# A decoder layer's kernel: first-norm squares on ScalarE, low parts on VectorE, weight sums in a fixed order, two more warming matmuls

## Chip, cores and metric

One core of one Trainium2 chip runs the kernel. The metric is the device time of one execution in microseconds (us), lower is better; each kernel is given by the median of its runs.

## What is computed

One decoder layer serves 528 prompt tokens (512 and 16 learned meta tokens) and 32 sample tokens, 560 columns in all; everything is fp32. Cut to what matters here:

```python
def swiglu(x, w_gate, w_up, w_down):
    return (jax.nn.silu(x @ w_gate) * (x @ w_up)) @ w_down

h = x + 0.5 * swiglu(rmsnorm(x, ffn1_norm), ffn1_w_gate, ffn1_w_up, ffn1_w_down)
n = rmsnorm(h, mix_norm)
# attention over a compressed cache for the one half of the heads, a
# causal convolution for the other, and one output projection
h = h + mix
h = h + 0.5 * swiglu(rmsnorm(h, ffn2_norm), ffn2_w_gate, ffn2_w_up, ffn2_w_down)
y = rmsnorm(h, final_norm)
```

The model width is 1024 and the hidden width of each FFN 2816, that is 22 hidden tiles of 128.

## The kernel before

**Stages.** The first FFN runs from the start to about 420 us, the mixers (projections, attention, convolution, output projection) to about 793 us, the second FFN to about 1180 us. Activations lie transposed, features on partitions and tokens along the row. A tile of 560 tokens (544 in the second FFN) goes to TensorE (PE) in two halves of 280 (272).

**Split products.** An fp32 product is made of three matmuls: the weights are split into a high part `wh`, a copy that ScalarE (ACT) rounds, and a low part `wl`, the weights less `wh`; the tokens likewise (`xs` and `xc`, two parts in one tile). The matmuls are high by high, high by low and low by high. There are three buffers each for `wh` and `wl`. In `w_split` (L272) the copy is L286 and the low part L287, on GpSimd (POOL).

**Plain hidden tiles.** Each FFN takes its hidden tiles in groups of 8, 7 and 7, and behind each group adds the down projection of the group to `h`. The first 5 tiles of the first FFN and the first 4 of the second are plain: gate and up times all 8 token tiles, 96 matmuls a tile; `evict` multiplies by the norm's factor (L184), takes silu (L752) and the product `hv` (L756), and splits it into `hid`: high part on ACT (L757), low part on POOL (L758). During them `Combos` (L594) makes the token combinations that the other tiles need: normed tokens `xn` (L621), sums `xt` (L627), and their splits `xc` (ACT L607, VectorE, DVE, L608).

**Seven-product units.** The other 17 and 18 hidden tiles, 35 units, use a Strassen-like scheme (`seven_unit`, L649): seven products m0 to m6 of 12 matmuls each take the place of eight. Four of the seven weight operands are tiles as loaded or corner differences, three are sums kept in the tile `ws`. `seven(i, m)` (L292) splits the operand of product m (`wh` on ACT L299, `wl` on DVE L300) and then makes the next sum on DVE (L308): sum 0 is `ws = a21 + a22`, sum 1 `ws -= a11`, sum 2 `ws = a12 - ws`, sum 3 `a11 -= a21`. Product 1 uses `ws` after sum 0, product 2 after sum 1, product 3 after sum 2; product 4 uses a11 after sum 3. PSUM results that a later product adds to are copied out first: `snap` (ACT, tile `sn`, L668) after products 0, 1 and 2. At a unit's end stand additions (DVE L672), silu (ACT L691), `hv` (two halves, DVE L696) and the split of `hid` (ACT L698, DVE L699).

**Order of the work.** The program emits its instructions piece by piece and a scheduler sets their order on each engine, by its own estimate of durations; a manual dependency without a semaphore (`add_manual_dep`) only fixes an order. On the chip each engine then works off its own queue in that order. SyncE issues the weight loads.

**First norm.** The start makes the split of the 8 token tiles (`feed`: ACT L542, DVE L543), and the sum of their squares in `Split.square`: squares of even tiles on POOL (L510) and of odd ones on ACT (L512), added on DVE (L521). The matmuls of the first hidden tiles need only the split tokens; from the sum, `rsqrt` (L425, p1 on PE L430, Newton step L462 to L466) and `spread` (L474, p2 on PE L481, copies to `rb` L483 and L485) make the norm's factor, which every eviction of a plain tile and every `xn` waits for. `NORM0` sets after how much of the plan's time PE turns to p1. `warm` (L468) runs matmuls on constants before the first weights are there.

Of the kernel before, what the change touches and what calls it, by code (L numbers as in the profile page):

```python
# [7 lines left out]
F32 = mybir.dt.float32  # L8
# [7 lines left out]
KD = 8  # L16
# [27 lines left out]

NORM0 = 12.5
NORM_LAT = 2.2
# [64 lines left out]
def kernel(  # L111
# [95 lines left out]
    def col(c):  # L207
        return par[:, c:c + 1]


    stream = []

    first_new = set()

    def add_w(ap, n):
        stream.append((ap, n))

    def add_ffn(gu, dn, apart=0, plain=NF):
        f0 = 0
        for nf in GROUPS:  # L220
            for f in range(f0, f0 + nf):
                if f == plain:
                    first_new.add(len(stream))
                add_w(gu[f], 2048 if f < plain else 0)
            for d in range(KD - (apart if f0 + nf == NF else 0)):
                add_w(dn[d, :, 128 * f0:128 * (f0 + nf)], 128 * nf)
            f0 += nf

    add_ffn(f1_gu, f1_d, 0, PLAIN1)
    for c in PLAN:  # L230
# [6 lines left out]
    for d, e in [(d, 1) for d in range(KD)] + [(d, 0) for d in range(KD)]:  # L237
        add_w(w_out_t[d, :, 512 * e:512 * e + 512], 512)
    add_ffn(f2_gu, f2_d, 2, PLAIN)

# [32 lines left out]
    def w_split(upto):  # L273
        while st["split"] < min(upto, len(subs)):
# [11 lines left out]
            nc.scalar.activation(out=hi, in_=raw, func=AF.Copy)  # L286
            nc.gpsimd.tensor_tensor(out=lo, in0=raw, in1=hi.bitcast(F32), op=ALU.subtract)  # L287
            splits[j] = (hi, lo)
# [3 lines left out]
    def seven(i, m):  # L292
# [213 lines left out]

    def square(part, after=None, pool=False):
        sq = Tm([128, part.shape[-1]], "sq")
        if pool:
            ins = nc.gpsimd.tensor_tensor(out=sq, in0=part, in1=part, op=ALU.mult)  # L510
        else:
            ins = nc.scalar.activation(out=sq, in_=part, func=AF.Square)  # L512
        if after is not None:
            tc.add_manual_dep(ins.ins, after.ins.name, mybir.DependencyInfo(
                mybir.DependencyClass.NoSync, mybir.DependencyReason.DATA), reason="the products wait for less")
# [11 lines left out]
    def hk(k):  # L527
        return hs[k // 2][:, k % 2]

    class Split:  # L530
# [9 lines left out]
        def feed(self, k, square=True):  # L540
            xk = U("x", [128, 2, self.n], F32R, "xs")
            fed = nc.scalar.activation(out=xk[:, 0], in_=hk(k), func=AF.Copy, scale=col(self.g + k))  # L542
            nc.vector.scalar_tensor_tensor(  # L543
                out=xk[:, 1], in0=hk(k), scalar=col(self.g + k), in1=xk[:, 0].bitcast(F32), op0=ALU.mult, op1=ALU.subtract
            )
            self.x[k] = xk
            if square:
                self.square(k)
            return fed

        def square(self, k, after=None, pool=False):
            self.ssum = accumulate(self.ssum, hk(k), after, pool)
            if k == KD - 1 and self.g != P_FIN:
# [95 lines left out]
    def seven_unit(w, cb, n, hid):  # L649
# [44 lines left out]
        for a, ps in ((0, b1), (1, b2)):  # L694
# [3 lines left out]
        nc.scalar.activation(out=x[:, 0], in_=hv, func=AF.Copy)  # L698
        lo = nc.vector.tensor_tensor(out=x[:, 1], in0=hv, in1=x[:, 0].bitcast(F32), op=ALU.subtract)  # L699
        tc.add_manual_dep(lo.ins, last_sum[0].ins.name, mybir.DependencyInfo(  # L700
            mybir.DependencyClass.NoSync, mybir.DependencyReason.DATA), reason="the next products wait for the sum")
        hid.append(x)

    def ffn(xs, hook, tail=None, plain=NF):
# [7 lines left out]
        for gi, nf in enumerate(GROUPS):  # L712
            hid = []
            for f in range(nf):
# [9 lines left out]
                for kh in range(2):  # L724
                    for j in range(2):
# [3 lines left out]
                        for k in range(4 * kh, 4 * kh + 4):  # L729
# [4 lines left out]
                            if plain < NF and xs.ev.ready:  # L734
# [580 lines left out]
    def main():  # L1315
# [461 lines left out]
```

## Time and profile before

| | |
|---|---|
| runs | 1204.67, 1199.27, 1201.39 us; median 1201.39 |
| profiled execution | 1197.67 us, its span 1195.9 us |
| mean granted clock of TensorE | 0.976 of full speed |
| busy: PE | 1133.9 us (95%) |
| DVE | 792.3 us (66%) |
| ACT | 535.0 us (45%) |
| POOL | 379.2 us (32%) |
| chain that ended last | PE 80%, DVE 10%, issue 3% |

The span is from the first to the last instruction; the profiled execution's own time is 1.8 us more. Busy is the share of the span in which an engine had an instruction under way. Matmuls overlap, so a busy PE can still be a PE that runs below its best pitch. The chain is followed back from the last instruction, at each step to what released it.

### The profile page before, as it was taken

Reading aid. Unit: us, or ns where it says so; the run is one execution under the profiler, and the core shown is the slowest. Engines: PE = TensorE matmul, PEld = TensorE weight load, DVE = VectorE, ACT = ScalarE, POOL = GpSimd, SP = SyncE. Lnnn points to the kernel's source line nnn. Section 1 sums busy time; section 2 is a strip of 40 time slices with the busy share of each in tenths; the row PEclk is TensorE's granted clock in tenths of the full one; section 3 lists DMA queues with packets and bytes.
Section 4 is the critical chain, followed back from the end, with each engine's and each line's share of the span. In section 5 each row is a group of like instructions: output and inputs, shape, how many; then the busy total and the mean of one; then the engine's idle time right before and its main releaser. Section 6 shows DMA issues by size and latency. Waiting matters only on the chain.

```text
span 1195.9 us, 24540 instructions
## 1 busy us (share of the span) xinstructions
PE 1133.9 (95%) x9314; PEld 1032.3 (86%) x9314; DVE 792.3 (66%) x1537; ACT 535.0 (45%) x1119; POOL 379.2 (32%) x374
## 2 busy tenths in 40 slices
PE   7999999999999999987889999999899999999995
PEld 7989999999999987876545556999899999999994
DVE  6898138834884346999877465659981598168824
ACT  4445226533655414432534555444552355245631
POOL 5440420033004545577434323444214100410141
PEclk8999999999999989998979999999899999999997
DMA  4151322332226656987869884223233233323222
GB/s 159 63 167 61 108 65 84 107 111 78 89 74 211 199 175 196 305 262 232 272 224 315 308 286 158 80 89 98 89 125 90 68 106 102 101 66 104 67 69 75
DMA packets 91062, 168.60 MB, mean 141 GB/s; under 512 B 18976, under 2 KB 25120, under 8 KB 90944
## 3 DMA queue, kind: packets, MB, share of 16 engines
q1 hardware_dynamic: 88352, 162.27, 42.4%
q0 software_dynamic: 2048, 4.20, 1.2%
q8 instruction: 74, 1.21, 0.4%
q10 hardware_dynamic: 544, 0.56, 0.1%
q14 instruction: 44, 0.36, 0.1%
HBM read 161.33 MB, written 5.65 MB: 140 GB/s over the span
## 4 chain that ended last, share of the span: by engine, by line
PE 80%; DVE 10%; issue 3%; ACT 2%; DMA 2%; POOL 2%; SPq 0%; another core or an unknown queue 0%; DVEq 0%; POOLq 0%; ACTq 0%
PE mm L349 36%; PE mm L661 31%; PE sc L1045 3%; PE ob L1067 2%; PE po L1292 2%; PE s L1236 2%; DVE cacc L917 1%; PE pt L1276 1%; DVE xc L608 1%; POOL wl L287 1%; PE mm L1607 1%; DVE wl L300 1%; DMA out<-glu 1%; PE p L481 1%; DVE xt L627 1%
## 5 line engine op out<-in xcount | busy, mean ns | idle before, releaser
L287 POOL TENSOR_TENSOR wl<-wr,wh 128x512 fp32r<-128x512 f32 (+1 forms) x177 | 229.9, 1301 | 541.8 <-ACT wh L286 530.7
L661 PE MATMUL mm<-xc,wh 128*128 128x272 f32 (+1 forms) x1960 | 371.9, 290 | 1.1 <-ACT wh L299 0.9
L661 PEld LDWEIGHTS mm<-xc,wh 128*128 128x128 f32 x1960 | 306.6, 188 | 1.8 <-ACT wh L299 1.3
L661 PE MATMUL mm<-xc,wl 128*128 128x272 f32 (+1 forms) x980 | 281.5, 293 | 3.6 <-DVE wl L300 3.6
L349 PE MATMUL mm<-hid,wh 128*128 128x280 f32 (+1 forms) x1352 | 226.9, 289 | 1.8 <-ACT wh L286 1.8
L286 ACT ACTIVATE wh<-wr 128x512 fp32r<-128x512 f32 (+1 forms) x177 | 107.9, 612 | 251.7 <-PE mm L349 194.9
L349 PEld LDWEIGHTS mm<-hid,wh 128*128 128x128 f32 x1352 | 192.6, 188 | 2.0 <-ACT wh L286 2.0
L661 PEld LDWEIGHTS mm<-xc,wl 128*128 128x128 f32 x980 | 182.2, 188 | 9.8 <-DVE wl L300 9.8
L349 PE MATMUL mm<-xs,wh 128*128 128x280 f32 (+2 forms) x992 | 181.8, 303 | 8.5 <-DVE xs L543 3.5
L349 PEld LDWEIGHTS mm<-xs,wh 128*128 128x128 f32 (+1 forms) x992 | 150.5, 196 | 14.0 <-DVE xs L543 4.2
L782 DVE SCALAR_TENSOR_TENSOR h<-mm,h 128x280 f32<-128x280 f32 (+1 forms) x92 | 36.8, 441 | 165.9 <-PE mm L349 165.9
L349 PE MATMUL mm<-hid,wl 128*128 128x280 f32 (+1 forms) x676 | 140.9, 290 | 0.0
L349 PE MATMUL mm<-xs,wl 128*128 128x280 f32 (+2 forms) x496 | 114.3, 305 | 6.1 <-POOL wl L287 6.0
L299 ACT ACTIVATE wh<-ra 128x512 fp32r<-128x512 f32 x140 | 87.8, 629 | 71.5 <-PE mm L661 62.8
L349 PEld LDWEIGHTS mm<-hid,wl 128*128 128x128 f32 x676 | 106.4, 188 | 0.0
L300 DVE TENSOR_TENSOR wl<-ra,wh 128x512 fp32r<-128x512 f32 x140 | 99.7, 715 | 3.9 <-ACT wh L299 1.1
L299 ACT ACTIVATE wh<-ws 128x512 fp32r<-128x512 f32 x105 | 66.2, 630 | 76.5 <-DVE ws L308 36.3
L349 PEld LDWEIGHTS mm<-xs,wl 128*128 128x128 f32 (+1 forms) x496 | 83.2, 196 | 10.3 <-POOL wl L287 8.7
L300 DVE TENSOR_TENSOR wl<-ws,wh 128x512 fp32r<-128x512 f32 x105 | 73.7, 702 | 26.9 <-ACT wh L299 24.3
L917 DVE SCALAR_TENSOR_TENSOR cacc<-glu,par,cacc 128x512 f32<-128x512 f32 x120 | 89.9, 749 | 1.5
L998 POOL DMA_INDIRECT rope<-in_pool_r,pr_sb x64 | 63.7, 996 | 46.4 <-PE sc L1045 33.5
L668 ACT ACTIVATE sn<-mm 128x272 f32<-128x272 f32 (+1 forms) x105 | 40.9, 390 | 29.2 <-PE mm L661 29.2
(247 smaller groups left out, 1514.4 us busy)
## 6 DMA issues: line engine op xcount, KB each, us to landing
page<-in_pool_c SPq DMA_DIRECT2D x256, 256.0 KB
ra<-in_f_gu SPq DMA_DIRECT2D x70, 512.0 KB
wr<-in_f_d SPq DMA_DIRECT2D x62, 256.0 KB
wr<-in_f_gu SPq DMA_DIRECT2D x36, 256.0 KB
wr<-in_w_in_t SPq DMA_DIRECT2D x24, 256.0 KB
wr<-in_f_d SPq DMA_DIRECT2D x30, 192.0 KB
wr<-in_w_out_t SPq DMA_DIRECT2D x16, 256.0 KB
h<-in_x_t SPq DMA_DIRECT2D x8, 280.0 KB
```

The costliest lines, as they stand in the source:

```text
L286: nc.scalar.activation(out=hi, in_=raw, func=AF.Copy)
L287: nc.gpsimd.tensor_tensor(out=lo, in0=raw, in1=hi.bitcast(F32), op=ALU.subtract)
L299: nc.scalar.activation(out=hi, in_=w, func=AF.Copy)
L300: nc.vector.tensor_tensor(out=lo, in0=w, in1=hi.bitcast(F32), op=ALU.subtract)
L349: nc.tensor.matmul(out=ps[a][:m, 0:n], lhsT=w, rhs=x[:, a * n:(a + 1) * n], start=first and o == 0 and j == 0, stop=last and o == 1,)
L661: nc.tensor.matmul(out=ps, lhsT=w_[:, c], rhs=x, start=first and k == 0 and j == 0, stop=k == 3 and j == 2, skip_group_check=True)
L668: nc.scalar.activation(out=s, in_=src, func=AF.Copy)
L782: last = halves(lambda o, i, x: nc.vector.scalar_tensor_tensor(out=o, in0=i, scalar=0.5, in1=x, op0=ALU.mult, op1=ALU.add), hk(d), ps, hk( ...
L917: last_tap = nc.vector.scalar_tensor_tensor(out=ps, in0=g[:, tp:S0 + tp], scalar=w, in1=ps, op0=ALU.mult, op1=ALU.add)
L998: last = nc.gpsimd.indirect_dma_start(out=rope[:, pg], out_offset=None, in_=pool_r, in_offset=bass.IndirectOffsetOnAxis(ap=pr_sb[:, 32 * g ...
L1045: nc.tensor.matmul(out=ps[32 * b:32 * b + 32], lhsT=w[:, g, 32 * b:32 * b + 32], rhs=x, start=(i_ == 0), stop=(i_ == 2), tile_position=(0, ...
L1067: nc.tensor.matmul(out=ob[32 * b:32 * b + 32, :], lhsT=pts[:, 128 * pg + 32 * b:128 * pg + 32 * b + 32], rhs=tiles[b][:, pg, 0:256], start ...
```

## The change

Five edits. `NORM0` goes from 12.5 to 15.5 and `warm(12)` to `warm(14)`. The squares of the first norm are all made on ACT, behind the split of the last token tile, and their additions on DVE stand behind the last low part of the tokens. Of the plain tiles' weights, those of tiles 2 to 4 of the first FFN and 1 to 3 of the second (`prepared`, 12 low parts in each FFN) get their `wl` on DVE, not on POOL, and so do the low parts of those tiles' `hid` (3 in each). The last three calls of `cb.last` (the last token combinations) come a little earlier. In the seven-product units a new helper, `behind`, fixes one order on DVE: every low part behind the previous sum, and every sum behind the low part emitted before it, so `last_sum` is now a chain through all of them.

```diff
-NORM0 = 12.5
+NORM0 = 15.5
...
+    def behind(ins, *others):
+        for o in others:
+            if o is not None:
+                tc.add_manual_dep(ins.ins, o.ins.name, mybir.DependencyInfo(
+                    mybir.DependencyClass.NoSync, mybir.DependencyReason.DATA), reason="the order in which the products need them")
+        return ins
...
-    def add_ffn(gu, dn, apart=0, plain=NF):
+    def add_ffn(gu, dn, apart=0, plain=NF, skip=0):
...
+                if skip <= f < plain < NF:
+                    prepared.add(len(stream))
                 add_w(gu[f], 2048 if f < plain else 0)
...
-    add_ffn(f1_gu, f1_d, 0, PLAIN1)
+    add_ffn(f1_gu, f1_d, 0, PLAIN1, 2)
...
-    add_ffn(f2_gu, f2_d, 2, PLAIN)
+    add_ffn(f2_gu, f2_d, 2, PLAIN, 1)
...
             nc.scalar.activation(out=hi, in_=raw, func=AF.Copy)
-            nc.gpsimd.tensor_tensor(out=lo, in0=raw, in1=hi.bitcast(F32), op=ALU.subtract)
+            eng = nc.vector if subs[j][0] in prepared else nc.gpsimd
+            eng.tensor_tensor(out=lo, in0=raw, in1=hi.bitcast(F32), op=ALU.subtract)
...
         nc.scalar.activation(out=hi, in_=w, func=AF.Copy)
-        nc.vector.tensor_tensor(out=lo, in0=w, in1=hi.bitcast(F32), op=ALU.subtract)
+        last_sum[0] = behind(nc.vector.tensor_tensor(out=lo, in0=w, in1=hi.bitcast(F32), op=ALU.subtract), last_sum[0])
...
-            last_sum[0] = nc.vector.tensor_tensor(out=out, in0=x, in1=y, op=op)
+            last_sum[0] = behind(nc.vector.tensor_tensor(out=out, in0=x, in1=y, op=op), last_sum[0])
...
-    def square(part, after=None, pool=False):
+    def square(part, after=None):
         sq = Tm([128, part.shape[-1]], "sq")
...
+        behind(nc.scalar.activation(out=sq, in_=part, func=AF.Square), after)
         return sq
...
-            nc.vector.tensor_tensor(out=sq, in0=s, in1=sq, op=ALU.add)
+            behind(nc.vector.tensor_tensor(out=sq, in0=s, in1=sq, op=ALU.add), lo)
...
-                                if f_all == plain and kh == 1 and k in (5, 7) and (j, k) != (1, 7):
-                                    cb.last({(0, 5): 1, (0, 7): 2, (1, 5): 3}[j, k], "x")
+                                if f_all == plain and kh == 1 and j == 0 and k > 4:
+                                    cb.last(k - 4, "x")
...
-                    nc.gpsimd.tensor_tensor(out=x[:, 1], in0=hv, in1=x[:, 0].bitcast(F32), op=ALU.subtract)
+                    eng = nc.vector if w.i in prepared else nc.gpsimd
+                    eng.tensor_tensor(out=x[:, 1], in0=hv, in1=x[:, 0].bitcast(F32), op=ALU.subtract)
...
         for k in range(KD):
-            xs.square(k, fed[min(k + 2, KD - 1)], k % 2 == 0)
+            xs.square(k, fed[KD - 1])
...
-    warm(12)
+    warm(14)
```

Each row of the order below is one instruction: line, operation, output, inputs, size. Numbers behind a name tell buffers and tiles apart; they and the lines of the changed kernel are shifted a little.

ACT, second seven-product unit of the first FFN, before. Here `wh_1266` (from `ws_1228`) is the high part for product 2, `wh_1295` for product 3, `wh_1316` for product 4, `wh_1336` for product 5; `sn_1302` is the copy after product 0, `sn_1322` after product 1, `sn_1342` after product 2.

```order
L691 ACTIVATE gu_1139<-gu_1139 128x560
L299 ACTIVATE wh_1266<-ws_1228 128x512
L698 ACTIVATE hid_1276<-hv_1273 128x560
L668 ACTIVATE sn_1302<-mm_1279 128x280
L668 ACTIVATE sn_1322<-mm_1280 128x280
L299 ACTIVATE wh_1295<-ws_1228 128x512
L299 ACTIVATE wh_1316<-ra_1089 128x512
L299 ACTIVATE wh_1336<-ra_1091 128x512
L668 ACTIVATE sn_1342<-mm_1279 128x280
```

The same stretch of the changed kernel, where product 2 has `wh_1268`, product 3 `wh_1297`, product 4 `wh_1318`, and the copies are `sn_1304`, `sn_1324` and `sn_1344`.

```order
L698 ACTIVATE gu_1141<-gu_1141 128x560
L675 ACTIVATE sn_1304<-mm_1281 128x280
L705 ACTIVATE hid_1278<-hv_1275 128x560
L312 ACTIVATE wh_1268<-ws_1230 128x512
L675 ACTIVATE sn_1324<-mm_1282 128x280
L312 ACTIVATE wh_1297<-ws_1230 128x512
L675 ACTIVATE sn_1344<-mm_1281 128x280
L312 ACTIVATE wh_1318<-ra_1091 128x512
L312 ACTIVATE wh_1338<-ra_1093 128x512
```

The copy after product 0 has moved from behind the two splits to ahead of them: the splits of `hid` and of product 2's weights now stand behind it. Of the 35 units 29 have the first order before and the second order after.

DVE in the same unit, before: `wl_1267`, `wl_1296` and `wl_1317` are the low parts for products 2, 3 and 4; L308 are sums 1, 3 and 2 in the order of the rows.

```order
L696 TENSOR_TENSOR hv_1273<-gu_1139,mm_1137 128x280
L308 TENSOR_TENSOR ws_1228<-ws_1228,ra_1089 128x512
L696 TENSOR_TENSOR hv_1273<-gu_1139,mm_1136 128x280
L308 TENSOR_TENSOR ra_1089<-ra_1089 128x512
L300 TENSOR_TENSOR wl_1267<-ws_1228,wh_1266 128x512
L308 TENSOR_TENSOR ws_1228<-ra_1091,ws_1228 128x512
L699 TENSOR_TENSOR hid_1276<-hv_1273,hid_1276 128x560
L300 TENSOR_TENSOR wl_1296<-ws_1228,wh_1295 128x512
L300 TENSOR_TENSOR wl_1317<-ra_1089,wh_1316 128x512
```

And now, with L321 the sums:

```order
L703 TENSOR_TENSOR hv_1275<-gu_1141,mm_1138 128x280
L703 TENSOR_TENSOR hv_1275<-gu_1141,mm_1139 128x280
L321 TENSOR_TENSOR ws_1230<-ws_1230,ra_1091 128x512
L313 TENSOR_TENSOR wl_1269<-ws_1230,wh_1268 128x512
L321 TENSOR_TENSOR ws_1230<-ra_1093,ws_1230 128x512
L706 TENSOR_TENSOR hid_1278<-hv_1275,hid_1278 128x560
L313 TENSOR_TENSOR wl_1298<-ws_1230,wh_1297 128x512
L321 TENSOR_TENSOR ra_1091<-ra_1091 128x512
L313 TENSOR_TENSOR wl_1319<-ra_1091,wh_1318 128x512
```

Sum 3 (`ra`), which stood ahead of product 2's low part, now stands behind product 3's, and so comes after sum 2.

DVE at the start, before, from the third split token tile (L543) to the last addition of squares (L521):

```order
L543 SCALAR_TENSOR_TENSOR xs_153<-h_124,par_76,xs_153 128x560
L543 SCALAR_TENSOR_TENSOR xs_156<-h_124,par_76,xs_156 128x560
L521 TENSOR_TENSOR sq_179<-sq_177,sq_179 128x560
L543 SCALAR_TENSOR_TENSOR xs_159<-h_129,par_76,xs_159 128x560
L543 SCALAR_TENSOR_TENSOR xs_162<-h_129,par_76,xs_162 128x560
L521 TENSOR_TENSOR sq_182<-sq_179,sq_182 128x560
L543 SCALAR_TENSOR_TENSOR xs_165<-h_132,par_76,xs_165 128x560
L521 TENSOR_TENSOR sq_185<-sq_182,sq_185 128x560
L543 SCALAR_TENSOR_TENSOR xs_168<-h_132,par_76,xs_168 128x560
L521 TENSOR_TENSOR sq_188<-sq_185,sq_188 128x560
L521 TENSOR_TENSOR sq_191<-sq_188,sq_191 128x560
L521 TENSOR_TENSOR sq_194<-sq_191,sq_194 128x560
```

And now (L550 and L528):

```order
L550 SCALAR_TENSOR_TENSOR xs_155<-h_126,par_76,xs_155 128x560
L550 SCALAR_TENSOR_TENSOR xs_158<-h_126,par_76,xs_158 128x560
L550 SCALAR_TENSOR_TENSOR xs_161<-h_131,par_76,xs_161 128x560
L550 SCALAR_TENSOR_TENSOR xs_164<-h_131,par_76,xs_164 128x560
L550 SCALAR_TENSOR_TENSOR xs_167<-h_134,par_76,xs_167 128x560
L550 SCALAR_TENSOR_TENSOR xs_170<-h_134,par_76,xs_170 128x560
L528 TENSOR_TENSOR sq_181<-sq_179,sq_181 128x560
L528 TENSOR_TENSOR sq_184<-sq_181,sq_184 128x560
L528 TENSOR_TENSOR sq_187<-sq_184,sq_187 128x560
L528 TENSOR_TENSOR sq_190<-sq_187,sq_190 128x560
L528 TENSOR_TENSOR sq_193<-sq_190,sq_193 128x560
L528 TENSOR_TENSOR sq_196<-sq_193,sq_196 128x560
```

The additions, which stood between the token splits, are all behind them. On POOL four squares of 128x560 are gone from this stretch, on ACT the eight squares stand behind the eight token splits and ahead of the fourth weight split.

## Rows read from the trace of the kernel before

**Rows 1.** The page's part 4: the chain that ended last, shares of the span by line.
```profile
PE mm L349 36%; PE mm L661 31%; PE sc L1045 3%; PE ob L1067 2%; PE po L1292 2%; PE s L1236 2%; DVE cacc L917 1%; PE pt L1276 1%; DVE xc L608 1%; POOL wl L287 1%; PE mm L1607 1%; DVE wl L300 1%; DMA out<-glu 1%; PE p L481 1%; DVE xt L627 1%
```

**Rows 2.** Busy time in five stretches; columns: PE, PEld, DVE, ACT, POOL, PEclk, DMA.
```profile
7.10:36.00 28.90, 24.84 (x154) 23.38 (x154) 21.68 (x20) 11.76 (x20) 18.82 (x12) 0.82 0.37 131
37.20:84.90 47.70, 45.07 (x337) 43.77 (x338) 46.32 (x65) 23.31 (x40) 24.40 (x16) 1.00 0.35 110
84.90:93.00 8.10, 6.06 (x43) 5.38 (x43) 6.53 (x12) 4.07 (x8) 1.38 (x1) 1.00 0.40 140
807.00:847.50 40.50, 36.72 (x263) 35.62 (x264) 39.83 (x60) 19.29 (x33) 18.85 (x12) 0.92 0.34 111
847.50:856.00 8.50, 6.11 (x44) 5.45 (x44) 7.71 (x14) 4.59 (x9) 1.34 (x1) 1.00 0.38 124
```

**Rows 3.** Timeline, ACT, one seven-product unit; columns: start us, us, engine, line, operation.
```profile
322.64 0.67 ACT L691 ACTIVATE gu<-gu 128x560 f32<-128x560 f32 x1
324.51 0.63 ACT L299 ACTIVATE wh<-ws 128x512 fp32r<-128x512 f32 x1 [1.20 <-DVE ws L308]
325.04 0.66 ACT L698 ACTIVATE hid<-hv 128x560 fp32r<-128x560 f32 x1
325.61 0.38 ACT L668 ACTIVATE sn<-mm 128x280 f32<-128x280 f32 x1
326.79 0.41 ACT L668 ACTIVATE sn<-mm 128x280 f32<-128x280 f32 x1 [0.80 <-PE mm L661]
327.09 0.62 ACT L299 ACTIVATE wh<-ws 128x512 fp32r<-128x512 f32 x1
...
333.67 0.67 ACT L691 ACTIVATE gu<-gu 128x560 f32<-128x560 f32 x1
```

**Rows 4.** Timeline, DVE, the same unit.
```profile
323.71 0.68 DVE L308 TENSOR_TENSOR ws<-ws,ra 128x512 f32<-128x512 f32 x1
...
324.67 0.68 DVE L308 TENSOR_TENSOR ra<-ra 128x512 f32<-128x512 f32 x1
325.27 0.69 DVE L300 TENSOR_TENSOR wl<-ws,wh 128x512 fp32r<-128x512 f32 x1
325.99 0.69 DVE L308 TENSOR_TENSOR ws<-ra,ws 128x512 f32<-128x512 f32 x1
...
327.75 0.69 DVE L300 TENSOR_TENSOR wl<-ws,wh 128x512 fp32r<-128x512 f32 x1 [0.41 <-ACT wh L299]
```

**Rows 5.** Timeline, PE and ACT, the first seven-product unit of the first FFN.
```profile
86.60 0.41 ACT L668 ACTIVATE sn<-mm 128x280 f32<-128x280 f32 x1 [0.86 <-PE mm L661]
87.95 0.41 PE L661 MATMUL mm<-xc,wh 128*128 128x280 f32 x2
88.15 0.40 ACT L668 ACTIVATE sn<-mm 128x280 f32<-128x280 f32 x1 [1.15 <-PE mm L661]
...
90.42 0.63 ACT L299 ACTIVATE wh<-ws 128x512 fp32r<-128x512 f32 x1
91.10 0.52 PE L661 MATMUL mm<-xc,wh 128*128 128x280 f32 x2 [0.43 <-ACT wh L299]
```

**Rows 6.** Timeline, the start: ACT, POOL and DVE until the first spread.
```profile
13.06 1.41 ACT L542 ACTIVATE xs<-h,par 128x560 fp32r<-128x560 f32 x2
13.45 4.78 POOL L510 TENSOR_TENSOR sq<-h 128x560 f32<-128x560 f32 x3
14.02 3.23 DVE L543 SCALAR_TENSOR_TENSOR xs<-h,par,xs 128x560 fp32r<-128x560 f32 x2
...
22.21 0.79 DVE L543 SCALAR_TENSOR_TENSOR xs<-h,par,xs 128x560 fp32r<-128x560 f32 x1
22.92 4.16 DVE L521 TENSOR_TENSOR sq<-sq 128x560 f32<-128x560 f32 x4
...
36.30 0.30 DVE L485 COPY rb<-p 128x140 f32<-128x140 f32 x1 [0.45 <-PE p L481]
```

**Rows 7.** Groups by line and form, 37.2 to 84.9 us, one of DVE's.
```profile
L608 DVE TENSOR_TENSOR xc<-xt,xc 128x560 fp32r<-128x560 f32 x7 | 9.0, 1293 | 0.4 <-ACT xc L607 0.3
```

More of the change, by code (lines that the diff above doesn't have):

```diff
@@ L208, in col @@
         return par[:, c:c + 1]
+    def behind(ins, *others):
[4 more added lines that the diff above has]
+        return ins
     stream = []
     first_new = set()
+    prepared = set()
     def add_w(ap, n):
         stream.append((ap, n))
-    def add_ffn(gu, dn, apart=0, plain=NF):
+    def add_ffn(gu, dn, apart=0, plain=NF, skip=0):
         f0 = 0
@@ L505, in rsqrt_after, with accumulate @@
         return ev
-    def square(part, after=None, pool=False):
+    def square(part, after=None):
         sq = Tm([128, part.shape[-1]], "sq")
[L509 to L515, printed above, removed]
-        return sq
-    def accumulate(s, part, after=None, pool=False):
-        sq = square(part, after, pool)
+        behind(nc.scalar.activation(out=sq, in_=part, func=AF.Square), after)
+        return sq
+    def accumulate(s, part, after=None, lo=None):
+        sq = square(part, after)
         if s is not None:
-            nc.vector.tensor_tensor(out=sq, in0=s, in1=sq, op=ALU.add)
+            behind(nc.vector.tensor_tensor(out=sq, in0=s, in1=sq, op=ALU.add), lo)
         return sq
@@ L542, in feed @@
             fed = nc.scalar.activation(out=xk[:, 0], in_=hk(k), func=AF.Copy, scale=col(self.g + k))
-            nc.vector.scalar_tensor_tensor(
+            self.lo = nc.vector.scalar_tensor_tensor(
                 out=xk[:, 1], in0=hk(k), scalar=col(self.g + k), in1=xk[:, 0].bitcast(F32), op0=ALU.mult, op1=ALU.subtract
@@ L549, in feed, with square @@
             return fed
-        def square(self, k, after=None, pool=False):
-            self.ssum = accumulate(self.ssum, hk(k), after, pool)
+        def square(self, k, after=None):
+            self.ssum = accumulate(self.ssum, hk(k), after, self.lo if after is not None else None)
             if k == KD - 1 and self.g != P_FIN:
@@ L698, in seven_unit @@
         nc.scalar.activation(out=x[:, 0], in_=hv, func=AF.Copy)
-        lo = nc.vector.tensor_tensor(out=x[:, 1], in0=hv, in1=x[:, 0].bitcast(F32), op=ALU.subtract)
-        tc.add_manual_dep(lo.ins, last_sum[0].ins.name, mybir.DependencyInfo(
-            mybir.DependencyClass.NoSync, mybir.DependencyReason.DATA), reason="the next products wait for the sum")
+        behind(nc.vector.tensor_tensor(out=x[:, 1], in0=hv, in1=x[:, 0].bitcast(F32), op=ALU.subtract), last_sum[0])
         hid.append(x)
@@ L745, in ffn, with evict @@
                             xs.x[k] = None
-                def evict(pair=pair, gu=gu):
+                def evict(pair=pair, gu=gu, w=w):
                     for j in range(2):
```

## The prediction

> **What bounds the kernel now.** I read the chain of waits first: its two largest entries are PE lines, L349 (plain tiles, down projections) and L661 (seven-product units), with 36% and 31% of the span [rows 1]. So time is lost or won where PE waits or runs at the lower clock, and I look for those places with the busy times by stretch. One product of a unit is 12 matmuls, and two copies out of PSUM behind successive products start at 86.60 and 88.15 [rows 5]: 1.55 us, .129 us a matmul. For the 272 columns of the second FFN I scale by 272/280 to .1254. Against that pitch each stretch shows its loss [rows 2]: 7.1 to 36 has 154 matmuls, 19.9 us of work in 28.9, so 9.0 lost, with PEclk .82; 37.2 to 84.9 has 337, 43.5 in 47.7, 4.2 lost; 84.9 to 93, 43, 5.5 in 8.1, 2.6 lost; 807 to 847.5, 263, 33.0 in 40.5, 7.5 lost, PEclk .92; 847.5 to 856, 44, 5.5 in 8.5, 3.0 lost. In the steady units little is lost: silu to silu takes 333.67 - 322.64 = 11.03 us [rows 3] for 84 matmuls, 10.84 us of work.
>
> **The fixed order in the units (the large term).** A manual dependency costs no wait by itself, but it moved other things: ACT now has the copy after product 0 ahead of the splits of `hid` and of product 2's weights. ACT works its queue in order, so both splits wait for product 0's end. In the trace they don't: `wh` for product 2 starts at 324.51, released by sum 1, and `hid` at 325.04; the copy after product 0 follows at 325.61 [rows 3]. Now I follow what hangs on that copy, in start-to-start times or with the gap to the next engine:
> - copy to `hid` .30 (326.79 to 327.09), `hid` to `wh` .57 (325.04 to 325.61) [rows 3];
> - `wh` .62 and .04 until the low part starts (327.09 to 327.71, then 327.75) [rows 3, 4];
> - low part to sum 2 .72 (325.27 to 325.99), the sum .69, and .12 until ACT starts on a sum (323.71 + .68 to 324.51) [rows 3, 4];
> - product 3's `wh` .62 + .04, its low part to sum 3 .60 (as 324.67 to 325.27), sum 3 .69 + .12 [rows 3, 4]: the part that is new in order, since sum 3 stood ahead of product 2's low part, at 324.67;
> - product 4's `wh` to product 5's .53 (324.51 to 325.04), that one .62, and .05 until PE starts (90.42 + .63 to 91.10) [rows 3, 5].
>
> The sum is 6.33 us from the start of one copy to the first matmul of product 5. In PE's order two matmuls of product 5 stand ahead of product 4's first low part, so behind that point come 2 of product 5, 10 of product 4, 10 of product 5, and the 24 of product 6 and the next unit's product 0: 46. The next copy starts .33 after the last one's start: product 2's first matmul is at 87.95, one pitch after product 1's last, and the copy at 88.15 [rows 5]. So the loop takes 6.33 + 45 x .129 + .33 = 12.47 us in the first FFN, 1.44 more than 11.03; in the second 6.33 + 45 x .1254 + .33 = 12.30 against 11.03 - 84 x .0036 = 10.73, 1.57 more. PE fills only the 38 other matmuls, 4.9 us, into the 6.33. The 29 units with the new order are 14 in the first FFN (two of the first group, six of each other) and 15 in the second: 14 x 1.44 + 15 x 1.57 = **43.7 us lost**. Bounds: nothing, if the loop doesn't bind; 2 us a unit, 58, if each of its 15 links is some .03 longer than its row. The nearest row takes my side: in the first unit, where the `wh` of product 3 stands behind a late `hid`, PE waits .43 for it [rows 5]. Queued behind the waiting copy are only these splits; weight loads are issued later by as much as PE is later, and DMA is under 40% busy in all five stretches but the change in order asks nothing more of it [rows 2].
>
> **The start.** Token low parts take .79 alone and 1.62 each (3.23 for two) while POOL squares (4.78 for three), and the additions stand between them [rows 6]; PE waits for them in the stretch that loses 9.0. With the squares off POOL and the additions behind, the low parts come nearer to ACT's pitch. ACT's token splits end at 14.47 (13.06 + 1.41) [rows 6]; without the two squares between them, .57 each as `hid` [rows 3], at 13.3, and eight squares (four of them new on ACT) at 17.9. The seven additions, .7 each, begin behind the low parts at 15.5 to 16.5 and end at about 21; now the last ends at 27.08 (22.92 + 4.16) [rows 6]. The factor follows 9.2 us after (36.30): about 6 us earlier. One low part of weights now stands ahead of the copy of the factor on DVE (.7), so I take **5.6 won**. It can't be more than the 9.0 lost there; at least it is 2, if the clock falls all the same: of the 28.9 us some 10 ran at half clock (.18 x 2 x 28.9), 1.2 GHz, behind PE's waits. `warm(14)` and `NORM0` are within that, as they fill or place PE work and add none to the path.
>
> The weight splits left on POOL still run beside the token splits. The trace has a low part 1.62 - .79 = .83 longer there, about half of a POOL square (1.59) [rows 6]. The Trainium skill, SBUF - State Buffer, section "Who interferes with whom", says that a VectorE instruction with two SBUF inputs, as this is, is blocked fully until a GpSimd instruction that reads SBUF is over. If that held, four low parts beside POOL would be later by four times 1.59 - .83, 3.0 us, and 2.6 would be left of the gain; the row decides for .83.
>
> **The plain tiles.** First FFN: POOL loses 12 low parts and 3 of `hid`, DVE gets them: 15 x .7 = 10.5 us on an engine busy 46.3 of 47.7 us [rows 2]. But its own work gets faster without POOL beside it: the seven `xc` in the row average 1.29 [rows 7], while a two-input operation of that size alone is the .79 of [rows 6]; .5 on each of the some 40 larger operations is 20 us. So DVE keeps ahead, and the waits for POOL go: **3.5 won** of 4.2 lost, and of the first unit's 2.6 **2.0**, as its sums come earlier. Bounds: all 6.8; or 8.8 lost, if POOL is no cause and DVE's 46.3 + 10.5 outruns the 48 (the added work not covered). Second FFN: 7 of the 7.5 lost go likewise, but the first weight sum of its first unit now stands behind the last `xc` on DVE, so that unit's loss roughly doubles, and more: **3.0 won** in all, from 0 to 7.
>
> **The sum.** 43.7 - 5.6 - 3.5 - 2.0 - 3.0 = 29.6 us slower than the profiled execution's 1197.67: 1227.3. The median of the runs, 1201.39, lies 3.7 above that execution; on its scale it is 1231, and I say **1230**. The mixers' orders hardly change; I give them 0, and 3 either way.
>
> **The rivals.**
> - *Faster: the loop doesn't bind.* If ACT reaches product 2's split before product 0 ends, as at 324.51 [rows 3], the units stay at 11.0 us, and the gains alone are left: 1201.4 - 14.1 = 1187. For it: the steady units have spare time on both ACT and DVE. It decides when the 6.33 us fall under the 4.9 that PE can fill, each link a quarter shorter than its row. Against it: the rows are unslowed ones, and the order of the queue is certain. 16%.
> - *No change: the loop binds in part.* If only some .5 us a unit are lost, because the low part of product 3 no longer holds sum 3 back as long, 29 x .5 = 14.5 eats the gains: 1195 to 1207. 8%.
> - *The clock falls in the units.* Each unit would have five short waits of PE, 1.6 us in all. In the second FFN's start the clock averages .92 over 40.5 us, 6.5 us at half, 3.3 us lost; once in each of six groups of tiles that is 20 us more, 1250. In the two first units with their 2.6 and 3.0 us of waits the clock stayed at 1.00, 2.4 GHz [rows 2]. 4%. The Trainium skill, TensorE: Matmul & The Clock Gate, section "A second HAM failure mode: psum-queue depth-cycling", tells of a kernel whose small gaps between groups of matmuls made the clock swing between its two levels; these two stretches don't show it.
> - *The plain tiles turn bad:* DVE becomes the bound there and the gains of 8.5 turn into some 9 lost: 1243 to 1248. 5%.
>
> **The numbers.** A measurement of this kernel tells about 0.5%, 6 us, from no change. My case (67%, 1214 to 1246), the clock and the plain tiles are slower: .76; no change .08; faster .16. The range 1194 to 1245 leaves out the faster case and the outer ends of the slower ones.
>
> **What would show it.** Right: silu to silu 12.3 to 12.5 us in the steady units, PE's waits there for ACT's `wh` and DVE's `wl` some 45 us in sum, where a unit now loses .2; the copy after product 0 waiting for PE, then `hid` and `wh` straight behind it; the factor of the first norm at about 30 us; token low parts at .8 us; no waits for POOL in the plain tiles. Wrong: silu to silu near 11.0, or product 2's `wh` done before product 0's end.

## The result, and the profile after

| | before | changed |
|---|---|---|
| median of the runs | 1200.56 us (1199.27 to 1204.67, 4 runs) | 1230.27 us (1227.02 to 1231.59, 4 runs) |
| profiled execution, span | 1197.67, 1195.9 us | 1231.59, 1229.8 us |

The ratio is 1.0237 (95% interval 1.0204 to 1.0271): slower, 29.7 us by the medians, 33.9 by the two spans. The page of the changed kernel, its chain by engine and three groups of its costliest lines (columns: operation, count, busy us, mean ns, idle time before it and what ended most of it):

```profile
PE 75%; DVE 11%; ACT 6%; issue 3%; DMA 2%; POOL 1%; SPq 0%; DVEq 0%; ACTq 0%; POOLq 0%
PE mm L362 38%; PE mm L668 24%; DVE wl L313 4%; PE sc L1051 3%; ACT wh L312 3%; PE ob L1073 2%; PE po L1298 2%; DVE ws L321 2%; PE s L1242 1%; DMA page<-in_pool_c 1%; PE pt L1282 1%; PE mm L1613 1%; ACT sn L675 1%; ACT hid L705 1%; PE v L1219 1%
...
L668 PEld LDWEIGHTS mm<-xc,wh 128*128 128x128 f32 x1960 | 308.3, 189 | 21.7 <-ACT wh L312 17.0
L668 PE MATMUL mm<-xc,wl 128*128 128x272 f32 (+1 forms) x980 | 285.3, 297 | 13.6 <-DVE wl L313 13.6
L668 PEld LDWEIGHTS mm<-xc,wl 128*128 128x128 f32 x980 | 183.3, 189 | 26.9 <-DVE wl L313 26.9
```

Against [rows 1] the seven-product matmuls (L668, formerly L661) hold 24% of the chain instead of 31%, and the five links of the forecast loop are in it: ACT `sn`, `hid` and `wh`, DVE `wl` and `ws`. PE's weight loads of the units now wait 17.0 us for ACT's high parts and 26.9 for DVE's low parts, together 43.9; in the kernel before the same two groups waited 1.3 and 9.8. One steady unit of the changed kernel on ACT, from the timeline:

```profile
328.03 0.66 ACT L698 ACTIVATE gu<-gu 128x560 f32<-128x560 f32 x1
329.93 0.40 ACT L675 ACTIVATE sn<-mm 128x280 f32<-128x280 f32 x1 [1.24 <-PE mm L668]
330.23 0.66 ACT L705 ACTIVATE hid<-hv 128x560 fp32r<-128x560 f32 x1
330.79 0.62 ACT L312 ACTIVATE wh<-ws 128x512 fp32r<-128x512 f32 x1
331.47 0.41 ACT L675 ACTIVATE sn<-mm 128x280 f32<-128x280 f32 x1
332.95 0.64 ACT L312 ACTIVATE wh<-ws 128x512 fp32r<-128x512 f32 x1 [1.07 <-DVE ws L321]
333.78 0.40 ACT L675 ACTIVATE sn<-mm 128x280 f32<-128x280 f32 x1 [0.19 <-PE mm L668]
335.01 1.67 ACT L312 ACTIVATE wh<-ra 128x512 fp32r<-128x512 f32 x3 [0.82 <-DVE ra L321]
337.94 0.63 ACT L312 ACTIVATE wh<-ra 128x512 fp32r<-128x512 f32 x1 [1.27 <-PE mm L668]
340.02 0.63 ACT L312 ACTIVATE wh<-ws 128x512 fp32r<-128x512 f32 x1 [1.44 <-DVE ws L321]
340.56 0.66 ACT L698 ACTIVATE gu<-gu 128x560 f32<-128x560 f32 x1
```

The copy at 329.93 waits 1.24 us for PE, `hid` and product 2's high part stand straight behind it, and silu to silu takes 340.56 - 328.03 = 12.53 us where [rows 3] had 11.03. On DVE, in the same unit, the sums and low parts follow one another, with waits for ACT between them:

```profile
329.48 0.69 DVE L321 TENSOR_TENSOR ws<-ws,ra 128x512 f32<-128x512 f32 x1
331.44 0.69 DVE L313 TENSOR_TENSOR wl<-ws,wh 128x512 fp32r<-128x512 f32 x1 [1.28 <-ACT wh L312]
332.17 0.69 DVE L321 TENSOR_TENSOR ws<-ra,ws 128x512 f32<-128x512 f32 x1
332.78 0.73 DVE L706 TENSOR_TENSOR hid<-hv,hid 128x560 fp32r<-128x560 f32 x1
333.62 0.69 DVE L313 TENSOR_TENSOR wl<-ws,wh 128x512 fp32r<-128x512 f32 x1
334.23 0.69 DVE L321 TENSOR_TENSOR ra<-ra 128x512 f32<-128x512 f32 x1
335.67 0.69 DVE L313 TENSOR_TENSOR wl<-ra,wh 128x512 fp32r<-128x512 f32 x1 [0.76 <-ACT wh L312]
```

Sum 1 is done at 330.17, yet product 2's low part starts at 331.44; in [rows 4] it started at 325.27, less than .9 us after sum 1. The forecast loop ends at the first matmul of product 5, whose weight load is this row:

```profile
336.21 0.30 PEld L668 LDWEIGHTS mm<-xc,wh 128*128 128x128 f32 x2 [0.22 <-ACT wh L312]
```

It starts 6.28 us after the copy at 329.93; the prediction's sum said 6.33. The stretches that answer to [rows 2], and the first of the tail (busy times of PE, PEld, DVE, ACT, POOL; PEclk; DMA share):

```profile
6.80:31.50 24.70, 21.78 (x155) 19.56 (x155) 16.50 (x22) 14.93 (x26) 11.77 (x8) 1.00 0.48 166
31.80:75.20 43.40, 43.14 (x320) 42.99 (x321) 41.35 (x78) 22.02 (x37) 5.66 (x2) 0.96 0.38 122
75.20:83.40 8.20, 8.20 (x66) 8.20 (x65) 6.73 (x13) 5.00 (x10) 0.00 (x0) 1.00 0.41 132
819.20:855.70 36.50, 34.48 (x271) 33.95 (x270) 36.01 (x72) 20.68 (x36) 4.66 (x1) 1.00 0.46 151
855.70:868.10 12.40, 11.24 (x70) 11.24 (x71) 10.00 (x17) 5.46 (x10) 0.00 (x0) 0.73 0.01 4
1165.90:1176.60 10.70, 8.88 (x59) 8.67 (x58) 2.49 (x5) 4.53 (x9) 6.69 (x6) 0.84 0.28 71
```

The start now does 155 matmuls in 24.7 us at the full clock, where it did 154 in 28.9 at .82. By the silu of the units, and the last matmuls of the first FFN and of the norm's spread in the second, the 33.9 us of span divide so: 9.5 won until the first unit's silu (97.65 to 88.12); 20.2 lost in the first FFN's units (the last silu 366.77 to 377.43); 2.0 lost in the mixers; 4.8 won in the second FFN's plain tiles and first unit (its factor to its first silu: 53.7 before, 48.9 now); 24.2 lost in its units (last silu 1133.93 to 1165.92); 1.9 lost in the tail.

### The profile page after: what moved, and what is told of

The parts are those of the page before. It is cut to its first block, busy times and chain, and to the rows that moved or that the text cites. A ratio compares the mean times of both kernels' runs of the same rounds, so it can differ in the third digit from the quotient of the medians.

```text
span 1229.8 us, 24524 instructions
## 1 busy us (share of the span) xinstructions
PE 1163.4 (95%) x9318; PEld 1039.5 (85%) x9318; DVE 777.7 (63%) x1567; ACT 539.3 (44%) x1123; POOL 330.5 (27%) x340
## 4 chain that ended last, share of the span: by engine, by line
PE 75%; DVE 11%; ACT 6%; issue 3%; DMA 2%; POOL 1%; SPq 0%; DVEq 0%; ACTq 0%; POOLq 0%
PE mm L362 38%; PE mm L668 24%; DVE wl L313 4%; PE sc L1051 3%; ACT wh L312 3%; PE ob L1073 2%; PE po L1298 2%; DVE ws L321 2%; PE s L1242 1%; DMA page<-in_pool_c 1%; PE pt L1282 1%; PE mm L1613 1%; ACT sn L675 1%; ACT hid L705 1%; PE v L1219 1%
## 5 line engine op out<-in xcount | busy, mean ns | idle before, releaser
L668 PE MATMUL mm<-xc,wh 128*128 128x272 f32 (+1 forms) x1960 | 392.6, 296 | 3.9 <-ACT wh L312 1.8
L300 POOL TENSOR_TENSOR wl<-wr,wh 128x512 fp32r<-128x512 f32 (+1 forms) x153 | 192.5, 1262 | 604.0 <-ACT wh L298 602.6
L668 PEld LDWEIGHTS mm<-xc,wh 128*128 128x128 f32 x1960 | 308.3, 189 | 21.7 <-ACT wh L312 17.0
L668 PE MATMUL mm<-xc,wl 128*128 128x272 f32 (+1 forms) x980 | 285.3, 297 | 13.6 <-DVE wl L313 13.6
L668 PEld LDWEIGHTS mm<-xc,wl 128*128 128x128 f32 x980 | 183.3, 189 | 26.9 <-DVE wl L313 26.9
L362 PE MATMUL mm<-xs,wh 128*128 128x280 f32 (+2 forms) x992 | 177.8, 299 | 3.5 <-ACT wh L298 1.8
L362 PEld LDWEIGHTS mm<-xs,wh 128*128 128x128 f32 (+1 forms) x992 | 147.4, 192 | 7.5 <-ACT wh L298 2.5
L313 DVE TENSOR_TENSOR wl<-ra,wh 128x512 fp32r<-128x512 f32 x140 | 95.2, 701 | 29.1 <-ACT wh L312 26.3
L312 ACT ACTIVATE wh<-ra 128x512 fp32r<-128x512 f32 x140 | 81.3, 624 | 71.6 <-PE mm L668 35.7
```

The lines of the kernel that those rows point to most:

```text
L300: eng.tensor_tensor(out=lo, in0=raw, in1=hi.bitcast(F32), op=ALU.subtract)
L313: last_sum[0] = behind(nc.vector.tensor_tensor(out=lo, in0=w, in1=hi.bitcast(F32), op=ALU.subtract), last_sum[0])
L362: nc.tensor.matmul(out=ps[a][:m, 0:n], lhsT=w, rhs=x[:, a * n:(a + 1) * n], start=first and o == 0 and j == 0, stop=last and o == 1,)
L668: nc.tensor.matmul(out=ps, lhsT=w_[:, c], rhs=x, start=first and k == 0 and j == 0, stop=k == 3 and j == 2, skip_group_check=True)
```

## Experiments

Each is timed against the kernel before on the same chip. The edits stand against the changed kernel if nothing else is said.

**1. No fixed order.**

```diff
-        last_sum[0] = behind(nc.vector.tensor_tensor(out=lo, in0=w, in1=hi.bitcast(F32), op=ALU.subtract), last_sum[0])
+        nc.vector.tensor_tensor(out=lo, in0=w, in1=hi.bitcast(F32), op=ALU.subtract)
...
-            last_sum[0] = behind(nc.vector.tensor_tensor(out=out, in0=x, in1=y, op=op), last_sum[0])
+            last_sum[0] = nc.vector.tensor_tensor(out=out, in0=x, in1=y, op=op)
```

> The change without the fixed order in the seven-product units (the low parts are no longer chained to the sums); all else stays. The units' order on ACT and DVE is then that of the kernel before in 29 of 29 units. Theory (the loop through ACT's copy after product 0 costs the time): silu to silu back at 11.0 and 10.75 us, the 44.4 us that the units and the 1.9 us that the last one lost are gone, 1230.3 - 46.3 = 1184; with the gains of the first 100 us and of the second FFN's start as measured (9.5 and 2.9) 1188. I expect 1185 to 1190. Rival 1 (only sum 3's new place behind product 3's low part costs the time): the same, 1188. Rival 2 (the work moved from POOL to DVE costs it): still about 1230.

Measured: 1189.24 us, ratio .9885 (.9831 to .9938), silu to silu 11.03 and 10.75 us as before. So the fixed order costs the whole loss, and the rest of the change is a gain. Rival 2 is out.

**2. Only the fixed order,** the same two lines and `behind` put into the kernel before.

> The kernel before with nothing but the fixed order in the seven-product units. Theory: silu to silu 12.5 and 12.3 us, 1200.6 + 46 = 1247. Rival 1: the same. Rival 2: 1200, no change.

Measured: 1237.66 us, ratio 1.0297 (1.0245 to 1.0350), silu to silu 12.53 and 12.34 us. The units lose what was said: from the first to the last silu 20.3 us in the first FFN and 24.3 in the second. The total is 9 us under the expectation because in this run the first unit comes 2.6 us earlier (silu at 95.06), first FFN's last silu to second FFN's first takes 489.0 us instead of 493.6, almost all of it in the mixers, which the edit doesn't touch, and the tail's 1.9 us don't come (62.0 us behind the last silu, as in the kernel before). Nor does the edit touch the start: up to 76 us all four engines have the order of the kernel before. But the clock differs, from 6 to 42 us .86 in the profile before and .95 in this one (first and second row, columns as above), and the factor's copy comes at 34.55 here, not at 36.30:

```profile
6.00:42.00 36.00, 30.23 (x194) 28.43 (x194) 26.45 (x30) 16.56 (x28) 21.20 (x14) 0.86 0.37 130
6.00:42.00 36.00, 29.30 (x206) 27.32 (x207) 27.67 (x31) 17.08 (x28) 22.67 (x15) 0.95 0.37 128
34.55 0.30 DVE L494 COPY rb<-p 128x140 f32<-128x140 f32 x1 [0.46 <-PE p L490]
```

So two profiles with the same order until then differ by 2.6 us at the first unit, and of the 9.5 us above so many need not be the change's.

**3. ACT's order put back,** the fixed order on DVE kept: the copy after product 0 goes behind product 2's high part and `hid`.

```diff
-        nc.scalar.activation(out=hi, in_=w, func=AF.Copy)
+        highs[m] = nc.scalar.activation(out=hi, in_=w, func=AF.Copy)
...
-        s1 = snap(b1)
+        s1 = snap(b1, highs[2], last_hid[0])
```

> The change with its fixed order on DVE, but on ACT the copy after product 0 put behind product 2's high part and the split of hid, by a manual order. Theory: the chain then starts at the end of the unit before (both hv, sum 1: 1.6 us behind it) and not at product 0's end; from there 5.5 us to product 5's first matmul, 7.1 us in which PE has 50 matmuls, 6.45: some .45 us a unit stay lost, period 11.5 and 11.2, so 1230.3 - 46 + 13 = 1197 to 1202. Rival 1 (sum 3's place): nothing changes on DVE, so 1230.

Measured: 1220.22 us, ratio 1.0152 (1.0102 to 1.0201), 12.02 and 11.95 us a unit. Neither theory holds. The copy is no longer waited for, but only a third of the loss in the first FFN goes. Its timeline shows why:

```profile
319.30 0.63 ACT L312 ACTIVATE wh<-ra 128x512 fp32r<-128x512 f32 x1 [1.27 <-PE mm L670]
321.38 0.63 ACT L312 ACTIVATE wh<-ws 128x512 fp32r<-128x512 f32 x1 [1.44 <-DVE ws L321]
```

```profile
319.97 0.69 DVE L313 TENSOR_TENSOR wl<-ra,wh 128x512 fp32r<-128x512 f32 x1
320.58 0.69 DVE L321 TENSOR_TENSOR ws<-ra 128x512 f32<-128x512 f32 x1
321.18 0.45 DVE L681 TENSOR_TENSOR gu<-mm,sn 128x280 f32<-128x280 f32 x1
322.04 0.69 DVE L313 TENSOR_TENSOR wl<-ws,wh 128x512 fp32r<-128x512 f32 x1 [0.42 <-ACT wh L312]
```

The next unit's first high part waits for PE (319.30: with three buffers it takes the one of product 4). Sum 0 now has to stand behind its low part, at 320.58, and product 1's high part waits 1.44 us for that sum. In the kernel before, sum 0 starts at 328.96 in the unit of [rows 3], 2.8 us ahead of the high part that answers to this one (331.77). From 319.30 the work goes through low part, sum 0, high and low part, `hv`, sum 1 to product 2's high part, 4.86 us (in the unit ahead from 307.27 to 312.13), then through the weights of products 3 to 5 to the end of product 4, which frees the buffer for the high part at 319.30. It is a second closed loop, 12.02 us long, hidden behind the first.

**4. Sum 3 free,** ACT's copy still ahead: the chain keeps sums 0 to 2 and leaves sum 3 out (`if m < 3:` ahead of the `behind`).

> The change with sum 3 alone taken out of the fixed order (it goes ahead of product 2's low part again on DVE); on ACT the copy after product 0 stays ahead of the splits in the 29 units. Theory: the loop is closed by product 3's low part and not by product 5's high part: 4.47 us from copy to product 3's first low matmul, 58 matmuls behind it, period 4.47 + 57 x .129 + .33 = 12.15 us in the first FFN and 11.95 in the second, 10 us less than the change: 1220. Rival 1: all the loss is gone, 1188.

Measured: 1214.98 us, ratio 1.0099 (1.0063 to 1.0135), 12.24 and 12.0 us a unit against 12.15 and 11.95 expected. Sum 3's place is worth the last .3 us of the loop and no more; rival 1 is out. Of the 5 us that the total lies under the expected 1220, 3 are between the first FFN's last silu and the second's first (487.7 us, in the changed kernel 490.7).

**5. ACT's copy behind, and sum 0 free** (the third edit, and `if m > 0:` ahead of the `behind`).

> As the run before with ACT's copy put behind, and sum 0 of the next unit taken out of the fixed order; sum 3 stays behind product 3's low part. Its trace showed a second loop that I had missed: product 4's end frees the buffer for the next unit's first high part, and from there its low part, sum 0, the next high and low part, both hv, sum 1 and product 2's high part follow one another (4.85 us), then 5.5 us to product 5: 12.02 us a unit. Theory of two loops: with sum 0 early this one is cut too, and product 5's weights come 6.4 us behind the end of the unit before, where PE has 6.45 us of work: silu to silu 11.05 to 11.2 us, 1190 to 1194. Rival (sum 3's place by itself makes what was left, 1220): still 12.0 us a unit and 1220.

Measured: 1200.29 us (1193.93 to 1208.73, 12 runs), ratio .9972 (.9946 to .9998), 11.33 and 11.12 us a unit. The second loop is cut, .7 and .8 us a unit go, and sum 3 is still in its fixed place. The units are .2 us longer than expected; with 29 of them that, and mixers that vary (below), make the 6 us above the expected range.

**6. Sum 0 free and nothing else** (`if m > 0:` alone).

> The change with sum 0 alone taken out of the fixed order and nothing forced on ACT. By the program's order ACT then has the copy after product 0 behind the splits in the 29 units, without any help, and DVE the order of the run with sum 0 free. Theory (the fixed place of the next unit's sum 0 both closes the second loop and made the scheduler turn ACT's order round): the same 11.35 and 11.1 us a unit as in that run, 1195 to 1202. Rival (the turn on ACT has another cause and the order alone does not tell): 12.0 us or more, 1215 and above.

Measured: 1199.74 us, ratio .9995 (.9967 to 1.0022), 11.33 and 11.12 us a unit, as expected. Freeing one sum takes some 30 of the 41 us between the changed kernel and experiment 1. Once sum 0 is early, the scheduler puts ACT's copy behind product 2's high part and `hid` by itself (they start at 319.10 and 319.64, the copy at 320.20); that it does so because it expects those weights earlier is argued, not shown. So both loops have one origin, the chain that puts the next unit's sum 0 behind a low part whose high part waits for a buffer. The .3 us a unit that are left are as much as sum 3's place made in experiment 4.

**7. Low parts of the plain tiles on POOL again,** no fixed order.

> The change without its fixed order and with the 30 low parts of the plain tiles back on POOL; the new first norm and warm(14) stay. Theory: of the 9.5 us won up to the first unit's silu the start makes 4.8 (the factor's copy at 31.49 instead of 36.30) and the low parts the other 4.7, and the second FFN's plain tiles 5: 1189 + 9 = 1196 to 1200. Rival (the gain is the squares' alone, the low parts cost on DVE what they free on POOL): 1189.

Measured: 1199.81 us, ratio .9966 (.9944 to .9987); first unit's silu at 91.73 (88.11 in the first experiment), factor to first silu in the second FFN 55.7 us (48.6). As they stand the low parts are worth 3.6 and 7.1 us here. The clock works on both: from 6 to 42 us it is 1.00 in this run and .95 in the first experiment, from factor to first silu .91 and .96, some 3 of the 7.1 us.

**8. The old first norm,** no fixed order: squares, `NORM0` and `warm` as before, low parts on DVE.

> The change without its fixed order and with the old first norm (squares on POOL and ACT between the token splits, NORM0 12.5, warm 12); the low parts stay on DVE. Theory: the factor comes at 36 us again, 4.8 us later, 1189 + 5 = 1194. Rival (DVE has so much room in the plain tiles that a late factor is made up): 1189.

Measured: 1189.19 us, ratio .9881 (.9853 to .9909). The factor's copy is at 33.65 us, in experiment 1 at 31.36, but the first unit's silu only 1.0 us later, at 89.15. So the rival holds in part: of the 2.3 us a little more than half is made up in the plain tiles once DVE has room there. That the totals of the two runs are the same owes as much to 2.8 us between the first FFN's last silu and the second's first (491.8 here, 494.6 there).

**9. Product 3's high part first,** no fixed order; `s5 = snap(b2, highs[3])` puts the copy after product 1 behind it.

> The change without its fixed order, and on ACT the copy after product 1 put behind the high part of product 3, which it precedes by .3 us in the kernel before and in the run without the fixed order. Theory: there product 3's low part is late by .2 us in each steady unit (11.03 us for 10.84 us of matmuls); with its high part .3 us earlier the wait goes, silu to silu 10.85 and 10.55 us, 29 x .2 = 5 to 6 us less than 1189: 1183 to 1184. Rival (the sum that the high part waits for ends no earlier, or the .2 us turn up at another product): 1189.

Measured: 1185.59 us, ratio .9852 (.9823 to .9881), but 11.07 and 10.87 us a unit, no shorter than 11.03 and 10.75. The rival holds for the units. ACT of this run:

```profile
317.26 0.64 ACT L312 ACTIVATE wh<-ws 128x512 fp32r<-128x512 f32 x1 [0.78 <-DVE ws L321]
317.80 0.62 ACT L312 ACTIVATE wh<-ra 128x512 fp32r<-128x512 f32 x1
318.32 0.39 ACT L676 ACTIVATE sn<-mm 128x280 f32<-128x280 f32 x1
```

The copy now ends at 318.71, and product 3, which writes the PSUM bank that it reads, starts at 318.76, .13 behind PE's pitch. The .3 us that the high part gains come back as a wait for the bank. What this run has below the first experiment arose in the mixers (its second FFN's factor is at 794.9, there at 803.3, with the first silu .3 apart), which the edit doesn't touch. Runs 1, 8 and 9 are all faster than both kernels, by 1.2 to 1.5% of the one before; which of them is the fastest their intervals do not tell.

## Why the prediction was right, point by point

- **The fixed order in the units: right in size.** Said 12.47 and 12.30 us, measured 12.52 and 12.33; said 43.7 us over all units, measured 20.2 + 24.2 = 44.4. Every link stood in the rows of before: copy to `hid` .30 there and .30 after (329.93 to 330.23), low part to sum 2 .72 and .73. From the copy to product 5's first matmul it was 6.28 us for the 6.33 said. PE's waits of 43.9 us answer to the some 45; in the unit shown they are 1.4 us, where the one of [rows 3] has .2. *Right in mechanism, not complete:* the loop through ACT's copy is the longest of the changed kernel, but a second one of 12.02 us lies behind it, and both come from the place of sum 0, which the prediction did not look at: it followed sum 3. Experiment 6 shows the origin. For the forecast only the longest loop counted. (Of the five DMA shares said to be under 40% one is .40 [rows 2]; nothing hangs on it.)
- **The start.** Said: factor 6 us earlier, 5.6 won. Measured: its copy at 31.49 instead of 36.30, 4.8, and clock 1.00 in the stretch; against the 34.55 of experiment 2, the same start at a better clock, it is 3.1. So part of the 4.8 is the low clock of the one profile before. The additions end at 23.04, not 21. DVE, and then POOL, of the changed kernel show the price of POOL's company once more:

```profile
11.22 1.43 DVE L550 SCALAR_TENSOR_TENSOR xs<-h,par,xs 128x560 fp32r<-128x560 f32 x1 [0.32 <-ACT xs L549]
13.29 0.79 DVE L550 SCALAR_TENSOR_TENSOR xs<-h,par,xs 128x560 fp32r<-128x560 f32 x1
19.65 1.65 DVE L528 TENSOR_TENSOR sq<-sq 128x560 f32<-128x560 f32 x1
21.40 1.64 DVE L528 TENSOR_TENSOR sq<-sq 128x560 f32<-128x560 f32 x1
```

```profile
10.40 1.66 POOL L300 TENSOR_TENSOR wl<-wr,wh 128x512 fp32r<-128x512 f32 x1
19.22 1.47 POOL L300 TENSOR_TENSOR wl<-wr,wh 128x512 fp32r<-128x512 f32 x1 [7.16 <-ACT wh L298]
20.66 1.78 POOL L300 TENSOR_TENSOR wl<-wr,wh 128x512 fp32r<-128x512 f32 x1
22.40 1.78 POOL L300 TENSOR_TENSOR wl<-wr,wh 128x512 fp32r<-128x512 f32 x1
24.54 1.29 POOL L300 TENSOR_TENSOR wl<-wr,wh 128x512 fp32r<-128x512 f32 x1 [0.36 <-ACT wh L298]
```

  Free of POOL a low part takes .79; the one at 11.22, beside POOL until 12.06, takes 1.43. The first five additions take .74 each, the last two, beside three weight splits, 1.65 and 1.64. I had counted the additions at .7 throughout. The prediction also took .83 in [rows 6], about half of a square's 1.59, as a sign against a full block. It is none: the two low parts there end at 17.25 and the three squares at 18.23, so in each 1.59 a low part has some .6 and a square some .98, one after the other (last section).
- **The plain tiles: the step that failed is the addition of the gains, with the start's in full.** I added 5.6, 3.5 and 2.0 to 11.1; measured are 9.5 until the first unit's silu, but this near match is luck: 2.6 of the 9.5 are between the profile before and experiment 2 (97.65 to 95.06), which have the same start. Against 95.06 the low parts alone bring 5.9 (89.15, experiment 8), where I had said 5.5, and both together 6.95 (88.11, experiment 1); in all three the clock is .95 from 6 to 42 us. So beside the low parts the first norm brings 1.0, where the sum has 5.6 and its lower bound 2. Alone it brings 3.3 (91.73, experiment 7), a part of it by the clock, 1.00 there. The rows are those of experiments 8 and 7:

```profile
6.00:42.00 36.00, 30.36 (x215) 28.22 (x215) 29.34 (x35) 17.58 (x30) 20.75 (x13) 0.95 0.37 130
6.00:42.00 36.00, 32.05 (x233) 29.39 (x233) 25.77 (x40) 21.61 (x37) 16.58 (x11) 1.00 0.39 131
```

  The factor came 3.1 us earlier than in experiment 2, not 6, and the sum took for granted that the first unit comes earlier by as much; a DVE with room catches up with a late factor (experiment 8). Both experiments contain the earlier `cb.last` calls, which no run takes back alone. That DVE has room is seen in the `xc` of [rows 7], 1293 ns in the mean before, and now:

```profile
L615 DVE TENSOR_TENSOR xc<-xt,xc 128x560 fp32r<-128x560 f32 x7 | 5.1, 731 | 0.9 <-ACT xc L614 0.9
```

  PE's waits for POOL until the end of the first unit, 1.9 us in the kernel before, are gone. In the second FFN 4.8 were won and 3.0 said.
- **The clock: the rival came, but not in the steady units.** In them, with five short waits each, the clock stayed at 1.00 (four units of the first FFN, same columns as in the stretches above):

```profile
186.20:236.30 50.10, 48.38 (x339) 44.24 (x338) 38.87 (x68) 25.71 (x50) 0.00 (x0) 1.00 0.26 85
```

  But in the second FFN's first unit it was .73 for 12.4 us (some 3.3 us lost), at the start of the tail .84 (1.7 us), and .96 in the first FFN's plain tiles, 31.80 to 75.20 (1.7 us). The first comes with two waits of PE; it is still 1.00 until 855.5 and .50 from 855.6 to 862.4:

```profile
854.96 0.53 PE L668 MATMUL mm<-xc,wh 128*128 128x272 f32 x2 [1.80 <-ACT wh L312]
856.86 0.59 PE L668 MATMUL mm<-xc,wl 128*128 128x272 f32 x1 [1.38 <-DVE wl L313]
```

  They are the late first sum that the prediction named, and stay without the fixed order (1.78 and 1.99 us in experiment 1, clock .86 in its 840.0:851.8). The tail's does not go with the fixed order: in the 10.7 us behind the last silu the clock is .84 in experiments 7 and 9 too, without the fixed order, and 1.00 in experiment 2, with it. Why it falls there is open, and the tail's 1.9 us can't be put down to the change.
- **The sum.** Said 29.6 us on the scale of the profiled execution, where it was 33.9; by the medians it was 29.7. The units' .7, the gains' 11.1 + 3.0 against 9.5 + 4.8, which nearly balance, and 2.0 and 1.9 us in the mixers and the tail that I had at nothing make the difference of 4.3. That the median came out at 1230.27 for 1230 is partly luck: the two profiled executions are 33.9 us apart, the mixers and the tail differ as much between kernels that are the same there, and the errors of the gains happen to balance.

## What to carry to other kernels

A manual order without a semaphore is not free: it pins an instruction behind one that may wait for a buffer, and the scheduler may turn the other engines' queues round as well. Before pinning, follow the chain through all engines until it closes on itself and compare its length with the work that the bound engine has meanwhile; then look for the second longest loop, since undoing one link of the longest gives back only the difference. Gains that free the same slack need not add, and a gain read against one execution holds that execution's clock: look for a second one with the same order.

## What the runs showed of the hardware that I had not expected

- The mixers, which no edit here touches beyond small shifts of order, took 391.4 to 402.1 us (from the first FFN's last matmul to the second's factor, 410.9 to 806.6 in the kernel before) in the profiles: 395.7 before, 397.7 changed, 402.1 in experiment 1, 391.4 in experiment 2; the prediction had given them 3 us either way. Their clock is .96 to .97, and PE's busy time is 367 to 371 us in all four:

```profile
401.20:803.30 402.10, 371.12 (x3439) 282.77 (x3437) 268.65 (x648) 174.54 (x467) 181.49 (x219) 0.96 0.69 222
```

```profile
428.60:820.00 391.40, 367.29 (x3432) 278.60 (x3430) 270.29 (x644) 175.43 (x467) 184.53 (x223) 0.97 0.70 228
```

  A mean lower by .01 over 400 us is 8 us at half clock, 4 us lost, so a part of the spread is time at 1.2 GHz; what makes one kernel spend more time there was not tried. It limits what a few us of difference between two such kernels can say.
- DVE, with two SBUF inputs, and POOL take turns, nearly to the full. The Trainium skill, SBUF - State Buffer, section "Who interferes with whom", has the later one fully blocked. The rows of the start agree with it to within .2 us: by that the low part at 11.22 would begin its .79 at 12.06, POOL's end, and end at 12.85; it ended at 12.65. The record of an instruction that is held up starts before its turn, so that its duration contains the wait; the ends tell the turns. DVE's low part and two additions end .59, .61 and .60 us behind POOL's ends at 12.06, 20.69 and 22.44, and POOL's splits end 1.14 behind each of the additions (21.30 to 22.44, 23.04 to 24.18). So a turn is some .60 of an addition's .74 or a low part's .79, and 1.14 of a split's 1.29 (the one at 24.54, with DVE idle): all but .1 to .2 us of each waits for the other. That a mere slowing of both would not keep the ends in such step is argued, not tried.
